# Hybrid attention and S5 layer, FFN: residual stores in GpSimd's queue, three operand splits on GpSimd, and a step of one pair as eight plain products

## The chip, the cores and the metric

The kernel runs on one core of a Trainium2 chip. The metric is the device time of one execution in microseconds (us), from the median of several runs. The engines are named as the profile names them: PE (TensorE matmuls, with PEld for its weight loads), DVE (VectorE), ACT (ScalarE), POOL (GpSimd) and SP (SyncE, which issues most DMAs).

## What is computed

One layer of a hybrid decoder on 1024 prompt positions and 8 sample positions (1032 columns in all), width 1024, with a feed-forward width of 2816. The part that matters here comes after the merge of the two branches:

```python
x = x + merged @ w_out
h2 = rms_norm(x, norm2_g)
x = x + (jax.nn.silu(h2 @ w_ffn_gate) * (h2 @ w_ffn_up)) @ w_ffn_down
y = rms_norm(x, norm_f_g)
```

All of it is float32 in and out. The kernel keeps everything transposed: 128 features on the partitions and the 1032 positions along the free axis.

## The kernel before

**Arithmetic.** Each float32 operand is split into a rounded high part (a cast to fp32r on ACT) and the rest, the low part (a subtraction, on DVE as a rule), and a product is three matmuls: high times high, high times low, low times high. So a weight block becomes usable in three steps: SP loads it (`wr_...`), ACT casts it (`wh_...`), DVE subtracts (`wl_...`). The casts and subtractions write to rings of three buffers, the raw blocks to rings of three (`wraw`) or seven (`hsm`).

**Positions.** They are cut into two stretches s = 0 and 1 of 516 columns (`SC`), each of two halves of 258 (`HC`). A matmul here has 258 columns.

**Output projection, `wout(s)`.** For each of eight row blocks m: two weight loads, the residual `xres`, 48 matmuls, the sum in `X1[m]` (tile `mg`) on DVE, its square on ACT, the sum of squares `s2`, and a DMA of the stretch of `X1[m]` to the DRAM tile `x1d`, which is read again in the last part. In the code before, SP issues that DMA, so in SP's queue it stands between the loads of the following weight blocks. `operands(s)` then scales `X1` in place by the norm (L1178), forms the sums `ts` and splits them into the operands `ho`. `wout(1)` runs woven with `operands(0)`, and `light(0)`, the first products of the FFN for stretch 0, with `operands(1)`.

**Seven products.** The two FFN projections and the down projection are computed in 2x2 blocks by a scheme of seven products for eight (`seven`, `products`): four row blocks of weights a11, a12, a21, a22, three sums and differences of them on POOL (`ws1` to `ws4` are four instructions), seven splits on ACT and DVE, and seven evictions of PSUM into the result. `combine` makes the seven right-hand sides of the down projection out of the four blocks of the hidden layer b11, b12, b21, b22; `spill` writes them to DRAM (`hid0` to `hid6`).

**Down projection.** `STEP` groups the eleven pairs of hidden row blocks into six steps, the last of which, step 5, has one pair (pair 1). `load_step(h)` reads the step's seven right-hand sides back (`hr`, a ring of three buffers) and splits them (`do`: a high part on ACT, a low part on DVE). `DOWN` lists which rows m of the result take which steps: `(2, 0, 1)` and `(3, 0, 1)` come first (tiles `d02`, `d03`), with step 1 loaded meanwhile, and `(2, 5, 6)` and `(3, 5, 6)` (tiles `d52`, `d53`) are the step of one pair for the rows m = 2 and 3; then come `(0, 4, 6)` and the last row, `(1, 4, 6)`. `down_after` adds each product to `X` on DVE, and where a row is done it squares it on ACT, sums the squares on POOL (tile `s`, 128x1032) and scales it on ACT.

**What sets the order.** Each engine runs its own queue in order. The queues are laid out at build time by a scheduler that simulates the program, so an edit at one place can exchange instructions around it.

Of the kernel before, what the change touches and what calls it, by code (L numbers as in the profile page):

```python
# [29 lines left out]
SC = 516  # L30
# [27 lines left out]
def body_(ctx, tc, h, o):  # L58
# [972 lines left out]
    hidd = [[dram.tile([128, SC], F32, tag=f"hid{i}_{f}", name=f"hid{i}_{f}") for f in range(NP)] for i in range(7)]  # L1031
    x1d = [dram.tile([128, T], F32, tag=f"x1d{m}", name=f"x1d{m}") for m in range(KD)]
# [106 lines left out]
    def wout(s):  # L1139
        cs = stretch(s)  # L1140
        for m in range(KD):
# [14 lines left out]
            SY.dma_start(x1d[m][:, cs], X1[m][:, cs])  # L1156
# [48 lines left out]
    def spill(f, U, ts, sl):  # L1205
        for i, src in enumerate(combine(U, ts, (P, V, P, V))):
            SY.dma_start(hidd[i][f].rearrange("p (s t) -> p s t", s=2)[:, sl], src)

# [117 lines left out]
    def load_step(h_):  # L1326
# [3 lines left out]
        for i in (range(7) if h_ != 1 else (2, 4, 6, 0, 3, 5, 1)):  # L1330
# [3 lines left out]
            for k in range(n):  # L1334
                SY.dma_start(t[:, k], hidd[i][fs[k]].rearrange("p (s t) -> p s t", s=2))
            tags = POS[h_ % 2]
            if n == 1:
                o_ = buf(tags[i], f"do{nm}", F32R, (128, 2, 2, HC))
                hi, lo = o_[:, 0:1], o_[:, 1:2]
            else:  # L1340
                hi, lo = (buf(tags[2 * i + e], f"do{nm}{'hl'[e]}", F32R, (128, 2, 2, HC)) for e in range(2))
            ops[h_, i] = hi, lo
            S.copy(hi, t[:, 0:n])
            V.tensor_tensor(lo, t[:, 0:n], f32(hi), op=ALU.subtract)
# [8 lines left out]

    sqs = {}
    started = []

    def down_after(m, last):
        xa, xb = tok(X[m]), tok(X[m + 4])

        def run(i, ps, sl):  # L1360
# [3 lines left out]
            if last and i >= 5:  # L1364
                j = m + 4 * (i - 5)
                if m != LASTM:
                    if not started:
                        started.append(j)
                        S.activation(s3, X[j], AF.Square)
                    else:  # L1370
                        sq = buf("s2", f"sq3{j}")
                        S.activation(sq, X[j], AF.Square)
                        P.tensor_tensor(s3, s3, sq, op=ALU.add)
                    S.activation(X[j], X[j], AF.Copy, scale=gf[:, j:j + 1])
                else:
                    s = sl.start
                    sqs[s, j] = small(f"sq3{j}{s}").rearrange("p a b -> p (a b)")
                    S.activation(sqs[s, j], X[j][:, stretch(s)], AF.Square)
# [66 lines left out]
    for n, (m, a, b) in enumerate(DOWN):  # L1445
# [6 lines left out]
        nm = f"d{a}{m}"  # L1452
        products(seven(down_rows(m, fs), 128 * len(fs), nm), down_op(a, b), (0, 1), nm,
# [122 lines left out]
```

## Time and profile before

| | |
|---|---|
| median of 3 runs | 1423.12 us (1421.62 to 1427.08) |
| profiled execution, its time | 1422.4 us |
| its span, first to last instruction | 1420.6 us |
| mean granted clock of PE | 0.972 of full speed |
| busy share PE, DVE, ACT, POOL | 95%, 64%, 40%, 33% |

Matmuls are pipelined and their ends are modelled, so PE's busy share hides small waits. The number of matmuls that began in a stretch of given length, beside the granted clock, tells more: a stretch where PE runs without a pause shows how many fit. A row of a timeline ends in brackets where its engine had been idle before it, with the time and what ended it.

### The profile page before, as it was taken

The page shows a single profiled execution, that of the slowest core. Times are in us where ns is not written, and L with a number is a line of the kernel's source. Part 1 is how long each engine was busy: PE and PEld are TensorE (multiplying, and loading weights), DVE is VectorE, ACT ScalarE, POOL GpSimd, SP SyncE. Part 2 cuts the span into 40 slices and gives each one's busy share as a digit, 9 for nine tenths or more (in the row PEclk, how much of TensorE's full clock was granted, in tenths as well). Part 3 has the DMA queues.
Part 4 walks back from the last instruction along what each step waited for, and adds up shares of the span by engine and source line. Part 5 has one row for each costly group of instructions (what it writes and reads, how often), then busy time and mean ns, then how long its engine had stood idle before and what let it go on. Part 6 is the DMA issues. An engine that isn't in the chain of part 4 may idle for free.

```text
span 1420.6 us, 25988 instructions
## 1 busy us (share of the span) xinstructions
PE 1342.8 (95%) x10019; PEld 1308.4 (92%) x10019; DVE 913.6 (64%) x1831; ACT 566.3 (40%) x1124; POOL 472.5 (33%) x431
## 2 busy tenths in 40 slices
PE   8999999987789999998899999999999979999995
PEld 7999999977689999997899999999999879999985
DVE  7968864389998545537394444444434896777593
ACT  6125655233236423334353333333334552344351
POOL 3033221266770001017063333333333552332153
PEclk9999999998789999999999999999999999999997
DMA  7230001211112011453443233323223863544113
GB/s 287 88 114 30 17 23 31 62 48 32 32 25 72 23 46 45 124 182 120 140 128 118 101 105 112 105 98 105 83 91 112 269 203 126 157 150 131 48 40 120
DMA packets 89931, 140.01 MB, mean 99 GB/s; under 512 B 16328, under 2 KB 33232, under 8 KB 89808
## 3 DMA queue, kind: packets, MB, share of 16 engines
q1 hardware_dynamic: 88448, 135.02, 30.1%
q0 software_dynamic: 640, 2.10, 0.4%
q8 instruction: 79, 1.29, 0.4%
q10 hardware_dynamic: 720, 1.23, 0.2%
q14 instruction: 44, 0.36, 0.1%
HBM read 104.90 MB, written 32.22 MB: 97 GB/s over the span
## 4 chain that ended last, share of the span: by engine, by line
PE 65%; DVE 12%; DMA 2%; issue 2%; POOL 1%; ACT 1%; SPq 0%; DVEq 0%; ACTq 0%; POOLq 0%
PE gs L130 2%; PE gs L128 2%; PE gs L129 2%; PE wo L130 2%; PE wo L128 2%; PE wo L129 2%; PE ps L128 1%; PE ps L130 1%; PE ps L129 1%; DVE mg L923 1%; PE pa L128 1%; PE pa L129 1%; PE pa L130 1%; DVE mg L1178 1%; DVE RE L873 1%
## 5 line engine op out<-in xcount | busy, mean ns | idle before, releaser
L130 PE MATMUL wo<-mh,wl_wo 128*128 128x258 f32 x256 | 74.0, 290 | 5.3 <-DVE wl_wo L118 5.3
L128 PE MATMUL wo<-mh,wh_wo 128*128 128x258 f32 x256 | 74.0, 289 | 2.4 <-ACT wh_wo L117 1.7
L129 PE MATMUL wo<-ml,wh_wo 128*128 128x258 f32 x256 | 73.2, 286 | 0.0
L130 PE MATMUL gs<-xh,wl_gs 128*128 128x344 f32 x192 | 62.2, 327 | 5.0 <-DVE wl_gs L118 5.0
L129 PE MATMUL gs<-xl,wh_gs 128*128 128x344 f32 x192 | 62.1, 324 | 0.0
L128 PE MATMUL gs<-xh,wh_gs 128*128 128x344 f32 x192 | 62.0, 324 | 0.0
L1094 POOL TENSOR_TENSOR ws_u<-wr_1u,ws_u 128x512 f32<-128x512 f32 x11 | 14.2, 1287 | 125.3 <-issue 125.3
L130 PEld LDWEIGHTS wo<-mh,wl_wo 128*128 128x128 f32 x256 | 49.5, 194 | 5.9 <-DVE wl_wo L118 5.9
L1094 POOL TENSOR_TENSOR ws_d<-wr_1d,ws_d 128x512 f32<-128x512 f32 (+3 forms) x14 | 15.3, 1090 | 117.6 <-DVE wl_3d L1081 56.5
L128 PEld LDWEIGHTS wo<-mh,wh_wo 128*128 128x128 f32 x256 | 49.9, 195 | 3.1 <-ACT wh_wo L117 3.1
L129 PEld LDWEIGHTS wo<-ml,wh_wo 128*128 128x128 f32 x256 | 49.7, 194 | 0.0
L118 DVE TENSOR_TENSOR wl_wo<-wr_wo,wh_wo 128x512 fp32r<-128x512 f32 x32 | 23.5, 735 | 39.8 <-ACT wh_wo L117 39.8
L130 PE MATMUL ga<-xh,wl_ga 128*128 128x344 f32 x144 | 47.1, 327 | 1.8 <-DVE wl_ga L118 1.8
L128 PE MATMUL ga<-xh,wh_ga 128*128 128x344 f32 x144 | 47.5, 330 | 0.0
L129 PE MATMUL ga<-xl,wh_ga 128*128 128x344 f32 x144 | 47.0, 326 | 0.0
L495 POOL TENSOR_TENSOR ml<-mg,mh 128x344 fp32r<-128x344 f32 x6 | 6.7, 1147 | 115.3 <-ACT mh L494 115.3
L130 PEld LDWEIGHTS gs<-xh,wl_gs 128*128 128x128 f32 x192 | 36.7, 192 | 5.2 <-DVE wl_gs L118 5.2
L577 ACT ACTIVATE P<-P,st 128x256 f32<-128x256 f32 (+1 forms) x64 | 31.0, 486 | 17.7 <-DVE st L574 17.7
L128 PEld LDWEIGHTS gs<-xh,wh_gs 128*128 128x128 f32 x192 | 36.6, 191 | 0.0
L117 ACT CAST wh_wo<-wr_wo 128x512 fp32r<-128x512 f32 x32 | 19.8, 619 | 42.2 <-PE wo L129 40.2
L129 PEld LDWEIGHTS gs<-xl,wh_gs 128*128 128x128 f32 x192 | 36.6, 191 | 0.0
L202 PE MATMUL u<-xh,wuh 128*128 128x344 f32 x96 | 30.8, 326 | 4.2 <-ACT wuh L220 4.0
(2689 smaller groups left out, 5863.1 us busy)
## 6 DMA issues: line engine op xcount, KB each, us to landing
hr<-hid SPq DMA_DIRECT2D x77, 258.0 KB, 3.5
wr_wo<-in_wout SPq DMA_DIRECT2D x32, 256.0 KB, 2.9
xres<-in_xT SPq DMA_DIRECT2D x16, 258.0 KB, 3.6
x1d<-mg SPq DMA_DIRECT2D x16, 258.0 KB, 2.8
x<-x1d SPq DMA_DIRECT2D x8, 516.0 KB, 4.7
wr_ga<-in_wst SPq DMA_DIRECT2D x16, 256.0 KB, 2.6
wr_gs<-in_wst SPq DMA_DIRECT2D x16, 256.0 KB, 2.6
wr_0g<-in_wfg SPq DMA_DIRECT2D x15, 256.0 KB, 3.0
```

The lines of the kernel that those rows point to most:

```text
L117: S.copy(wh[:, 0:w], raw[:, 0:w])
L118: (eng or V).tensor_tensor(wl[:, 0:w], raw[:, 0:w], f32(wh[:, 0:w]), op=ALU.subtract)
L128: TE.matmul(ps, wh, xh[:, cs], start=(k == 0), stop=False)
L129: TE.matmul(ps, wh, xl[:, cs], start=False, stop=False)
L130: TE.matmul(ps, wl, xh[:, cs], start=False, stop=(k == n - 1))
L202: TE.matmul(ps[:, :CH], wh, XH[k][:, chunk(c)], start=(k == 0), stop=False)
L495: eng.tensor_tensor(lo, src, f32(hi), op=ALU.subtract)
L577: S.activation(Pt[:, i, 0:W], Pt[:, i, 0:W], AF.Exp, bias=nm_[:, i:i + 1], scale=0.125, accum_out=ds[:, i:i + 1])
L873: V.tensor_tensor_scan(RE[:, gg], a, W1[:, gg], 0.0, op0=ALU.mult, op1=ALU.add)
L923: V.tensor_tensor(MG[m][:, chunk(c)], MG[m][:, chunk(c)], t, op=ALU.mult)
L1094: P.tensor_tensor(t, x, y, op=op)
L1178: V.scalar_tensor_tensor(x, x, g2[:, j:j + 1], r2[:, cs], op0=ALU.mult, op1=ALU.mult)
```

## The change

Four things are done.

1. In `wout`, the store of `X1[m]` to `x1d` is issued by POOL and not by SP.
2. In `load_step(1)`, the low parts of the right-hand sides 4, 0 and 5 are subtracted on POOL; the other four stay on DVE.
3. The step of one pair is no longer computed by seven products for the rows m = 2 and 3 (`d52`, `d53`) but by `plain`: eight products, four row blocks of weights as they are, two halves of columns, each output block the sum of two products in its own PSUM tile. No sum of weights is formed, there are four splits and four evictions for a row where there were seven of each, and the two rows take 96 matmuls of 258 columns where there were 84.
4. The plain products need b12, which the scheme of seven products does not keep: it is spilled for pair 1 to a new DRAM tile `h12` (one DMA for each stretch), and loaded and split as an eighth right-hand side of step 5.

```diff
-            SY.dma_start(x1d[m][:, cs], X1[m][:, cs])
+            P.dma_start(x1d[m][:, cs], X1[m][:, cs])
...
             SY.dma_start(hidd[i][f].rearrange("p (s t) -> p s t", s=2)[:, sl], src)
+        if f in STEP[-1]:
+            SY.dma_start(h12.rearrange("p (s t) -> p s t", s=2)[:, sl], U[1])
...
-        for i in (range(7) if h_ != 1 else (2, 4, 6, 0, 3, 5, 1)):
+        for i in (range(7 if n > 1 else 8) if h_ != 1 else (2, 4, 6, 0, 3, 5, 1)):
...
-                SY.dma_start(t[:, k], hidd[i][fs[k]].rearrange("p (s t) -> p s t", s=2))
+                SY.dma_start(t[:, k], (hidd[i][fs[k]] if i < 7 else h12).rearrange("p (s t) -> p s t", s=2))
...
             S.copy(hi, t[:, 0:n])
-            V.tensor_tensor(lo, t[:, 0:n], f32(hi), op=ALU.subtract)
+            (P if h_ == 1 and i in (4, 0, 5) else V).tensor_tensor(lo, t[:, 0:n], f32(hi), op=ALU.subtract)
...
+    def plain(m, a, after):
+
+        n = 128
+        nm = f"d{a}{m}"
+        w = []
+        for q, ld in enumerate(down_rows(m, STEP[a])):
+            t = raw512(f"{q}{nm}")
+            ld(t)
+            w.append(wsplit(t[:, 0:n], n, f"{q}{nm}"))
+            if q % 2 == 0:
+                continue
+            for c in range(2):
+                t = two(("b0", "b1", "b0", "b2")[q - 1 + c], f"{nm}{q}{c}")
+                for s in range(2):
+                    for e in range(2):
+                        i = ((0, 1), (7, 5))[c][e]
+                        mm(t[:, s, 0:HC], w[q - 1 + e], lambda k: tuple(x[:, 0, s] for x in ops[a, i]), e == 0, e == 1)
+                after(q // 2, c, t[:, :, 0:HC])
...
+    def plain_after(m):
+        def run(r, c, ps):
+            d = tok(X[m + 4 * r])[:, :, c]
+            V.tensor_tensor(d, ps, d, op=ALU.add)
+            if c:
+                squares(m, r, slice(0, 2))
+        return run
...
         nm = f"d{a}{m}"
+        if len(fs) == 1:
+            plain(m, a, plain_after(m))
+            continue
         products(seven(down_rows(m, fs), 128 * len(fs), nm), down_op(a, b), (0, 1), nm,
```

`squares` is what `down_after` did at the end of a row, moved into a function of its own.

The scheduler moves instructions at the places below. The first is ACT's queue in `wout(1)`, where the row blocks m = 5 and 6 (`wo51`, `wo61`, each loaded in a part 0 and a part 512) are cast between the high parts `ho` of `operands(0)`. Before:

```order
L1184 CAST ho2h0_7161<-ts20_7351 128x258
L1154 ACTIVATE sq231_7345<-mg3_2896 128x516
L1184 CAST ho6h0_7169<-ts20_7351 128x258
L1184 CAST ho3h0_7163<-ts30_7440 128x258
L117 CAST wh_wo51_512_7467<-wr_wo51_512_7465 128x512
L1184 CAST ho4h0_7165<-ts30_7440 128x258
L1184 CAST ho2h0_7161<-ts30_7440 128x258
L117 CAST wh_wo61_0_7529<-wr_wo61_0_7527 128x512
```

And with the change, on the same engine at the same place:

```order
L1185 CAST ho2h0_7162<-ts20_7352 128x258
L1155 ACTIVATE sq231_7346<-mg3_2896 128x516
L1185 CAST ho6h0_7170<-ts20_7352 128x258
L117 CAST wh_wo51_512_7468<-wr_wo51_512_7466 128x512
L1185 CAST ho3h0_7164<-ts30_7441 128x258
L117 CAST wh_wo61_0_7530<-wr_wo61_0_7528 128x512
L1185 CAST ho4h0_7166<-ts30_7441 128x258
L1185 CAST ho2h0_7162<-ts30_7441 128x258
```

The cast of the second part of block 5 now stands ahead of the first cast that reads `ts30`, and that of block 6 two places further ahead; DVE's subtractions for them move in the same way.

On POOL, at the same place, the sums `ts20` and their low parts stood in a row before:

```order
L1066 TENSOR_TENSOR ts10_7262<-mg5_2902,ts10_7262 128x258
L1067 TENSOR_TENSOR ts10_7262<-mg5_2902,ts10_7262 128x258
L1185 TENSOR_TENSOR ho2l0_7162<-ts10_7262,ho2h0_7161 128x258
L1185 TENSOR_TENSOR ho6l0_7170<-ts10_7262,ho6h0_7169 128x258
L1064 TENSOR_TENSOR ts20_7351<-mg2_2895 128x258
L1065 TENSOR_TENSOR ts20_7351<-mg6_2903,mg2_2895 128x258
L1066 TENSOR_TENSOR ts20_7351<-mg6_2903,ts20_7351 128x258
L1067 TENSOR_TENSOR ts20_7351<-mg6_2903,ts20_7351 128x258
L1185 TENSOR_TENSOR ho2l0_7162<-ts20_7351,ho2h0_7161 128x258
L1185 TENSOR_TENSOR ho6l0_7170<-ts20_7351,ho6h0_7169 128x258
L1064 TENSOR_TENSOR ts30_7440<-mg3_2896 128x258
```

With the change, POOL's queue there reads:

```order
L1067 TENSOR_TENSOR ts10_7263<-mg5_2902,ts10_7263 128x258
L1157 DMA x1d2_6452<-mg2_2895 128x516
L1068 TENSOR_TENSOR ts10_7263<-mg5_2902,ts10_7263 128x258
L1186 TENSOR_TENSOR ho2l0_7163<-ts10_7263,ho2h0_7162 128x258
L1186 TENSOR_TENSOR ho6l0_7171<-ts10_7263,ho6h0_7170 128x258
L1065 TENSOR_TENSOR ts20_7352<-mg2_2895 128x258
L1066 TENSOR_TENSOR ts20_7352<-mg6_2903,mg2_2895 128x258
L1067 TENSOR_TENSOR ts20_7352<-mg6_2903,ts20_7352 128x258
L1068 TENSOR_TENSOR ts20_7352<-mg6_2903,ts20_7352 128x258
L1157 DMA x1d3_6453<-mg3_2896 128x516
L1186 TENSOR_TENSOR ho2l0_7163<-ts20_7352,ho2h0_7162 128x258
L1186 TENSOR_TENSOR ho6l0_7171<-ts20_7352,ho6h0_7170 128x258
```

Two stores stand between the sums, one of them ahead of the last sum of `ts10`, the other ahead of the low parts of `ts20`.

The second place is SP's queue at the end of `wout(1)`, with the last residuals and the first weights of the FFN (`wr_0g000` and on). Before:

```order
L1156 DMA x1d5_6454<-mg5_2902 128x516
L1144 DMA xres61_7539<-in_xT 128x516
L1156 DMA x1d6_6455<-mg6_2903 128x516
L1144 DMA xres71_7607<-in_xT 128x516
L1156 DMA x1d7_6456<-mg7_2904 128x516
L1256 DMA wr_0g000_7666<-in_wfg 128x512
L1256 DMA wr_1g000_7672<-in_wfg 128x512
```

With the change, on SP at the same place:

```order
L111 DMA wr_wo71_512_7602<-in_wout 128x512
L1145 DMA xres61_7540<-in_xT 128x516
L1145 DMA xres71_7608<-in_xT 128x516
L1259 DMA wr_0g000_7667<-in_wfg 128x512
L1259 DMA wr_1g000_7673<-in_wfg 128x512
```

No instruction that waits for a result of DVE is left ahead of the first FFN weights in SP's queue.

The third place is DVE's queue at the start of the down projection (`d02`), where the low parts of step 1 (`do14l`, `do10l`, `do16l`) stand between the last products of the hidden layer (`A15`, `s2`), the weight splits and the evictions `x22`. Before:

```order
L1081 TENSOR_TENSOR wl_0d02_13254<-wr_0d02_13249,wh_0d02_13253 128x256
L1344 TENSOR_TENSOR do14l_13211<-hr14_13207,do14h_13210 128x1032
L1227 TENSOR_TENSOR A15_11_12839<-A15_11_12839,h6_11_12838 128x258
...
L1363 TENSOR_TENSOR x22_13134<-d02b0_13257,x22_13134 128x2x258
L1344 TENSOR_TENSOR do10l_13225<-hr10_13221,do10h_13224 128x1032
L1065 TENSOR_TENSOR s2_11_12840<-A15_11_12839 128x258
L1344 TENSOR_TENSOR do16l_13218<-hr16_13214,do16h_13217 128x1032
L1363 TENSOR_TENSOR x22_13134<-d02b1_13275,x22_13134 128x2x258
L1081 TENSOR_TENSOR wl_3d02_13315<-ws1_d02_13293,wh_3d02_13314 128x256
```

With the change, on DVE:

```order
L1082 TENSOR_TENSOR wl_0d02_13257<-wr_0d02_13252,wh_0d02_13256 128x256
L1230 TENSOR_TENSOR A15_11_12841<-A15_11_12841,h6_11_12840 128x258
...
L1066 TENSOR_TENSOR s2_11_12842<-A15_11_12841 128x258
L1082 TENSOR_TENSOR wl_2d02_13301<-ws2_d02_13298,wh_2d02_13300 128x256
L1409 TENSOR_TENSOR x22_13137<-d02b0_13260,x22_13137 128x2x258
L1068 TENSOR_TENSOR s2_11_12842<-A15_11_12841,s2_11_12842 128x258
L1347 TENSOR_TENSOR do16l_13221<-hr16_13217,do16h_13220 128x1032
L1409 TENSOR_TENSOR x22_13137<-d02b1_13278,x22_13137 128x2x258
L1082 TENSOR_TENSOR wl_3d02_13318<-ws1_d02_13296,wh_3d02_13317 128x256
```

`do14l` and `do10l` are gone from DVE's queue ahead of the fourth weight split, and the last sum `s2` of the hidden layer stands ahead of `do16l`. POOL takes `do14l` ahead of its first sum `s2`, `do10l` ahead of its weight sum `ws4`, and `do15l` after the weight sums of `d03`.

## Rows read from the trace of the kernel before

**Rows 1.** Page, part 1: busy time, share of the span, instructions.

```profile
PE 1342.8 (95%) x10019; PEld 1308.4 (92%) x10019; DVE 913.6 (64%) x1831; ACT 566.3 (40%) x1124; POOL 472.5 (33%) x431
```

**Rows 2.** Stretches: length, busy PE PEld DVE ACT POOL (x started), clock, DMA share, GB/s.

```profile
585.00:590.00 5.00, 5.00 (x44) 5.00 (x44) 1.98 (x3) 1.88 (x3) 0.00 (x0) 1.00 0.33 104
...
670.00:675.00 5.00, 5.00 (x30) 5.00 (x30) 3.52 (x5) 1.82 (x4) 1.83 (x3) 0.66 0.66 211
...
690.00:695.00 5.00, 2.38 (x15) 2.30 (x15) 2.10 (x6) 1.86 (x4) 0.00 (x0) 0.65 0.97 315
695.00:700.00 5.00, 5.00 (x31) 5.00 (x31) 1.02 (x4) 1.93 (x3) 0.00 (x0) 0.67 0.54 191
```

**Rows 3.** The same view in stretches of 10 us, down projection.

```profile
1160.00:1170.00 10.00, 6.03 (x39) 5.49 (x38) 9.40 (x13) 5.09 (x8) 6.45 (x6) 0.80 0.86 258
...
1190.00:1200.00 10.00, 10.00 (x86) 10.00 (x85) 4.95 (x8) 1.87 (x3) 5.16 (x4) 1.00 0.18 51
...
1350.00:1360.00 10.00, 7.95 (x56) 6.85 (x55) 9.33 (x18) 7.24 (x15) 5.13 (x6) 1.00 0.29 80
1360.00:1370.00 10.00, 8.86 (x63) 8.89 (x64) 9.83 (x14) 6.18 (x10) 5.53 (x4) 0.83 0.21 59
```

**Rows 4.** Chain of waits that ended last: start, us, engine, tile, line.

```profile
667.09 0.65 POOL ts L1064
668.08 0.62 ACT wh_wo L117
668.72 1.04 DVE wl_wo L118
...
688.31 4.00 DMA wr_0g<-in_wfg
```

**Rows 5.** PE's timeline around block 5 and at the FFN's start: start, us.

```profile
667.29 0.28 PE L130 MATMUL wo<-mh,wl_wo 128*128 128x258 f32 x1
668.75 0.39 PE L128 MATMUL wo<-mh,wh_wo 128*128 128x258 f32 x1 [1.17 <-ACT wh_wo L117]
668.97 0.28 PE L129 MATMUL wo<-ml,wh_wo 128*128 128x258 f32 x1
669.81 0.39 PE L130 MATMUL wo<-mh,wl_wo 128*128 128x258 f32 x1 [0.56 <-DVE wl_wo L118]
...
689.41 1.05 PE L157 MATMUL r2c<-ones,s 128*86 128x2 f32 x12 [2.28 <-DVE s L1155]
...
693.08 0.58 PE L1115 MATMUL xg<-ho0h,wh_0g 128*128 128x258 f32 x1 [2.62 <-ACT wh_0g L1080]
```

**Rows 6.** ACT's timeline, the cast ahead of block 5's second part.

```profile
667.76 0.41 ACT L1184 CAST ho3h<-ts 128x258 fp32r<-128x258 f32 x1 [2.51 <-POOL ts L1064]
```

**Rows 7.** POOL's timeline: a DMA that it issues, and its longest wait.

```profile
8.79 0.54 POOL L217 DMA_DIRECT2D wur<-in_wu  x1 [4.68 <-DVE wul L225]
...
653.52 4.91 POOL L1065 TENSOR_TENSOR ts<-mg,mg 128x258 f32<-128x258 f32 x1
```

**Rows 8.** Who PE waited for from 1105 to 1182 us: total, times, longest.

```profile
PE d02b L1117 <- DVE wl_3d L1081: 2.3, 1, 2.3
PE d02b L1115 <- DVE x L1363: 2.1, 2, 1.7
```

**Rows 9.** Timelines of DVE and POOL: a split of step 1, and a DVE split beside a POOL sum.

```profile
1157.01 1.22 DVE L1344 TENSOR_TENSOR do14l<-hr,do14h 128x1032 fp32r<-128x1032 f32 x1
...
1365.21 2.78 DVE L1081 TENSOR_TENSOR wl_2d<-ws_d,wh_2d 128x384 fp32r<-128x384 f32 x1
...
1365.05 2.52 POOL L1373 TENSOR_TENSOR s<-s,sq 128x1032 f32<-128x1032 f32 x1 [2.58 <-ACT sq L1372]
```

**Rows 10.** DVE's timeline in the step of one pair: a split, an eviction, an undisturbed 384 split.

```profile
1348.29 0.28 DVE L1081 TENSOR_TENSOR wl_2d<-ws_d,wh_2d 128x128 fp32r<-128x128 f32 x1
1348.48 0.69 DVE L1363 TENSOR_TENSOR x<-d52b,x 128x516 f32<-128x516 f32 x1
...
1364.28 0.55 DVE L1081 TENSOR_TENSOR wl_1d<-wr_1d,wh_1d 128x384 fp32r<-128x384 f32 x1
```

More of the change, by code (lines that the diff above doesn't have):

```diff
@@ L1031, in body_ @@
     hidd = [[dram.tile([128, SC], F32, tag=f"hid{i}_{f}", name=f"hid{i}_{f}") for f in range(NP)] for i in range(7)]
+    h12 = dram.tile([128, SC], F32, tag="h12", name="h12")
     x1d = [dram.tile([128, T], F32, tag=f"x1d{m}", name=f"x1d{m}") for m in range(KD)]
@@ L1334, in load_step @@
             for k in range(n):
-                SY.dma_start(t[:, k], hidd[i][fs[k]].rearrange("p (s t) -> p s t", s=2))
+                SY.dma_start(t[:, k], (hidd[i][fs[k]] if i < 7 else h12).rearrange("p (s t) -> p s t", s=2))
             tags = POS[h_ % 2]
             if n == 1:
-                o_ = buf(tags[i], f"do{nm}", F32R, (128, 2, 2, HC))
+                o_ = buf(tags[i] if i < 7 else ("r", "Zh3", "Zh2")[nraw[0] % 3], f"do{nm}", F32R, (128, 2, 2, HC))
                 hi, lo = o_[:, 0:1], o_[:, 1:2]
@@ L1352, in down_op, with squares @@
         return op
+    def plain(m, a, after):
[15 more added lines that the diff above has]
+                after(q // 2, c, t[:, :, 0:HC])
     sqs = {}
     started = []
+    def squares(m, i, sl):
+        j = m + 4 * i
+        if m != LASTM:
+            if not started:
+                started.append(j)
+                S.activation(s3, X[j], AF.Square)
+            else:
+                sq = buf("s2", f"sq3{j}")
+                S.activation(sq, X[j], AF.Square)
+                P.tensor_tensor(s3, s3, sq, op=ALU.add)
+            S.activation(X[j], X[j], AF.Copy, scale=gf[:, j:j + 1])
+        else:
+            s = sl.start
+            sqs[s, j] = small(f"sq3{j}{s}").rearrange("p a b -> p (a b)")
+            S.activation(sqs[s, j], X[j][:, stretch(s)], AF.Square)
+    def plain_after(m):
[5 more added lines that the diff above has]
+        return run
     def down_after(m, last):
@@ L1364, in run @@
             if last and i >= 5:
[L1365 to L1378, printed above, removed]
+                squares(m, i - 5, sl)
         return run
```

## The prediction

> **What bounds the kernel now.** I read the page's busy shares first [rows 1]: PE is busy for 95% of the span, so the other engines matter only where PE stands still or runs at half clock. The stretches show where. A full 5 us, 585 to 590, takes 44 matmuls of 258 columns [rows 2]; a full 10 us, 1190 to 1200, takes 86 [rows 3]: 0.116 us for one. Three places that the change touches fall short, and each has its own last wait.
>
> Place A is the second stretch of the output projection and the start of the FFN behind it. From 670 to 675 us PE began 30 matmuls at a mean clock of 0.66, from 690 to 700 us 15 and 31 at 0.65 and 0.67 [rows 2]; such a mean is a mixture of the two levels, 2.4 GHz (1.00) and 1.2 GHz (0.50), and each time PE had paused before it. The chain of waits runs there through a POOL sum, an ACT cast and a DVE split between 667 and 669 us [rows 4], and then through the landing of the first FFN weight, issued at 688.31 us and 4.00 us in coming. PE's timeline shows the two pauses that these end [rows 5]. Place B is the start of the down projection, 1160 to 1170 us: 39 of 86 matmuls, clock 0.80, DVE busy 9.40 of 10 us [rows 3]. The waits name DVE both times, once for a weight split and twice for evictions [rows 8]. Place C is the step of one pair, 1350 to 1370 us: 56 and 63 of 86 with DVE at 9.33 and 9.83 [rows 3].
>
> **Part 1, the stores, at block 5.** ACT's cast for block 5's second part stood behind a cast that waited 2.51 us for POOL's `ts30` [rows 6]. PE paused from 667.29 to 668.75 and from 668.97 to 669.81 us [rows 5], 2.30 us in all, of which two ordinary steps of 0.12 are work: 2.06 lost. In the new order the cast stands ahead of that wait, and only behind `ho6h` of `ts20`. Against that, POOL's queue has two stores among the sums. An issue took POOL 0.54 us [rows 7], and both sums that they store are on time, so the sums come up to 1.1 us later. I trace it through: the casts and the split are then ready some 0.5 us after PE wants them. So 1.5 us of the 2.06 come back. The half clock behind the pause cost 14 matmuls against 44 in 5 us, 1.6 us; with a quarter of the pause left I take 1.5 of it (0 to 1.6).
>
> **Part 1, at the FFN's start.** SP's queue no longer holds the store of block 7, which waited for DVE, ahead of `wr_0g000`. The load needs a free buffer of the ring of seven, and the one it takes was last read for block 4, three blocks earlier; so it lands under block 6 or 7. What is late next is the sum of squares: PE began its column sums at 689.41 us, after 2.28 us of waiting for DVE, and they take 1.05 us [rows 5]. So the first FFN product can start at 690.5 and not at 693.08: 2.6 us. DVE's first split stands behind a small operation on those column sums and ends some 0.9 us after them (0.2 and 0.7, as the 516 columns of [rows 10]), 0.4 late for PE's fifth matmul: 2.2 us remain. The half clock after 693.08 us costs 9 matmuls for 16 up to 695 us (the other 6 of the 15 are column sums) and 31 for 44 after it [rows 2], together 20 at 0.116, 2.3 us. The pause shrinks to a shorter one; I take 1.0 (0 to 2.3). The stores of the first stretch, and the last ones, find POOL idle and cost nothing. If POOL were busy there, 0.54 us each would count. The two further DMAs for `h12` and its load are three issues among SP's others, whose cover is the loads that wait for buffers anyway; 0. Without the cover they would cost about 1 us.
>
> Part 1 together: 1.5 + 1.5 + 2.2 + 1.0 = 6.2 us.
>
> **Part 2, the three splits.** DVE sheds three splits of 1.22 us [rows 9], 3.7 us in a stretch where it has no time left. POOL takes 2.52 us for an operation of that size, and the same rows show what DVE pays beside it: a split that takes 0.55 us alone [rows 10] took 2.78, from 1365.21 to just after POOL's end at 1367.57 us. So POOL's operation holds DVE's next split until it is over. The Trainium skill, SBUF — State Buffer, section Who interferes with whom, gives this as a rule: a DVE instruction with two SBUF inputs and a GpSimd instruction that reads SBUF contend for one exclusive lock, and the later one blocks until the first is done. That speaks against this part, and the trace agrees: 2.78 against 0.55 us; evictions, which read PSUM, are free of it (0.69).
>
> I walk the queues with these durations. `do14l` on POOL falls beside DVE's first weight split of `d02` and holds it until PE has waited some 0.8 us. `do10l` falls beside the sum `s2` and `do16l`, holds them for about 2.4 us, and the fourth weight split, for which PE waits now, comes some 1.8 us later than now. What comes back: the third eviction, for which PE waits 1.7 us [rows 8], no longer stands behind `do13l`, and two later evictions not behind `do11l` and `do15l`. By that count PE's fifth product starts about when it does now, and a shorter pause behind it goes. Net I take 0, between a loss of 2.5 (both holds, nothing back) and a gain of 3.7 (no hold).
>
> **Part 3, the plain products.** The stage loses 30 + 23 matmuls in 1350 to 1370 us [rows 3]: 53 x 0.116 = 6.1 us. The change adds 12 matmuls, 1.4 us. DVE drops six splits of 0.28 us and six evictions of 0.69 [rows 10], 5.8 us in a stage of 16, and POOL eight small sums. PE then is the longer side: 96 matmuls are 11.2 us, DVE's eight splits and eight evictions 7.8. What stays is one hold by POOL's sum of squares, up to 2.5 us [rows 9], since the last split of `d53` falls beside it; I take 2.4. Gain 6.1 - 1.4 - 2.4 = 2.3 us (1.0 to 4.7). The split of the eighth right-hand side, 0.7 us on DVE, falls under the last product of `d33`, where DVE still has pauses.
>
> **Sum.** Against the profiled execution, 1422.4 us: 1422.4 - 6.2 - 0 - 2.3 = 1413.9. The median of the runs shown, 1423.12, is 0.7 higher, so the forecast is 1414.5. A measurement of this kernel tells about 0.5% (7 us) from no change; the forecast is 8.6 below the median, close to that bound.
>
> **The rivals.** *Half of it.* Pauses get shorter but the clock falls as often as now, and in the step of one pair ACT, which squares and scales the finished rows between the casts, is the new wait, so that part 3 only pays for its own matmuls. For it: a pause of 2.3 us ahead of the column sums stays [rows 5], and a shorter one, 1.46 us, sufficed for the half clock of 670 to 675 us. Against it: ACT was busy 7.24 and 6.18 of 10 us [rows 3] and sheds six casts. Then 1422.4 - 1.5 - 2.2 = 1418.7, with the median 1419.
>
> *All of it.* DVE's splits find POOL's pauses, part 2 pays 3.7 us, no hold stays in part 3 (4.7), and the clock stays up (1.5 + 1.6 + 2.2 + 2.3): 16.0 us, so 1406.4. For it: DVE and POOL overlap without loss in many rows. Against it: rows 9.
>
> *Slower: the stores hold POOL.* POOL's longest operation of its kind, 4.91 us [rows 7], where another of these sums took 0.65 [rows 4], began just as DVE started a run of splits without a pause, and ended when DVE paused. If an issue is held like that, the stores of blocks 1, 2 and 3, which fall in that run, cost 3 x (4.9 - 0.5) = 13 us in the chain POOL, ACT, PE [rows 4], and a further half-clock stretch some 1.6 us: 1414.5 + 14.6 = 1429; from about 3.3 us a store the change is a loss. Against it: an issue at 8.79 us took 0.54 [rows 7].
> The same page of the Trainium skill, section SBUF: two separate sides, warns of this, and the section A bandwidth-pool intuition that's wrong has the figure: a DMA issued from GpSimd whose descriptors wait for DVE takes about 3.1 us where it takes 0.62 alone; by that figure three stores would cost 7.4 us (an estimate from the page) and the time would be about 1422. It ties this to a mode of DVE that its two-input operations don't have, and no row here shows a GpSimd issue beside busy DVE.
>
> **How the numbers follow.** Forecast 0.49, its own range 1410 to 1417. Half of it 0.24. All of it 0.14. Slower 0.13. Faster by over 0.5% is below 1416: 0.42 of the forecast's share and all of the third, 0.56. Slower by over 0.5% is above 1430: half of the fourth, 0.07. The rest, 0.37, is within 0.5%. The range 1408 to 1421 leaves out the fourth case and half of the third, 0.20.
>
> **What would show it.** Part 1: the first FFN product starts within 1.5 us of the column sums' end, no pause over 0.7 us in block 5, each store on POOL near 0.54 us. Wrong if stores take 2 us or more beside DVE, or if the first weight still lands last. Part 2: POOL's `do` rows near 2.5 us with DVE rows of 1.5 us or more beside them, and PE's matmuls of 1160 to 1170 us between 35 and 50 of 86. Part 3: the 96 matmuls of `d52` and `d53` in 12 to 14 us where the 84 took 16. The forecast is wrong altogether if one of the earlier gains turns up as a new wait later: in the last row, whose DVE is full.

## The result and the profile after

The changed kernel takes 1414.25 us, median of 4 runs (1413.53 to 1415.45), where the kernel before takes 1423.26: a ratio of 0.9934 with a 95% interval of 0.9913 to 0.9955, or 9.0 us. A second measurement, beside other runs of the kernel before, gives 1414.89 against 1421.93, ratio 0.9951 (0.9938 to 0.9964), or 7.0 us. The forecast was 1414.5, and 8.5 us for the sum.

Single executions of one kernel differ by more than a part of this change is worth: the kernel before ran from 1415.1 to 1427.4 us. The traces show one reason, and it matters for what follows: the stretches in which PE is granted half its clock do not fall at the same places in each execution. So the parts are read stage by stage, from several traces, and not from totals alone.

The page of the changed kernel, part 1, answers to [rows 1]:

```profile
PE 1340.5 (95%) x10031; PEld 1306.4 (92%) x10031; DVE 907.2 (64%) x1817; ACT 565.8 (40%) x1119; POOL 483.3 (34%) x442
```

PE has 12 matmuls more and 2.3 us less of busy time, since less of it runs at half clock. POOL is busy 10.8 us longer: it has sixteen stores and three splits more, and eight small sums fewer.

Place A, PE's timeline of the changed kernel around block 5 and at the FFN's start, answers to [rows 5]:

```profile
668.63 0.39 PE L130 MATMUL wo<-mh,wl_wo 128*128 128x258 f32 x1 [0.53 <-DVE wl_wo L118]
...
686.70 1.05 PE L157 MATMUL r2c<-ones,s 128*86 128x2 f32 x12 [2.27 <-DVE s L1156]
687.61 0.37 PE L1116 MATMUL xg<-ho0h,wh_0g 128*128 128x258 f32 x1
...
688.61 0.58 PE L1118 MATMUL xg<-ho0h,wl_0g 128*128 128x258 f32 x1 [0.28 <-DVE wl_0g L1082]
```

Of block 5's two waits, 1.17 and 0.56 us, one of 0.53 is left. The first FFN product follows the column sums without a wait; what remains there is 0.28 us for DVE's split. The pause of 2.27 us ahead of the column sums is what it was. POOL's timeline shows the stores that came into its queue, with a row of DVE's timeline that runs beside the second of them, and SP's timeline the first FFN weights:

```profile
658.88 0.57 POOL L1157 DMA_DIRECT2D x1d<-mg  x1
665.03 0.56 POOL L1157 DMA_DIRECT2D x1d<-mg  x1
...
664.41 1.23 DVE L118 TENSOR_TENSOR wl_wo<-wr_wo,wh_wo 128x512 fp32r<-128x512 f32 x1
...
671.22 0.56 POOL L1157 DMA_DIRECT2D x1d<-mg  x1
...
685.45 0.54 POOL L1157 DMA_DIRECT2D x1d<-mg  x1 [5.18 <-DVE mg L1150]
```

```profile
673.73 0.33 SPq L1259 DMA_DIRECT2D wr_0g<-in_wfg  x1
676.34 0.33 SPq L1259 DMA_DIRECT2D wr_0g<-in_wfg  x1
```

The first weight is issued at 673.73 us, under block 6, 14 us ahead of its use; before it was 688.31 [rows 4].

Place B, PE's pauses in `d02` and `d03` (answers to [rows 8]), then POOL's low parts of step 1 and the DVE rows that run beside them (answers to [rows 9]):

```profile
1153.13 0.39 PE L1118 MATMUL d02b<-do00h,wl_0d 128*128 128x258 f32 x1 [0.50 <-DVE wl_0d L1082]
1156.96 0.36 PE L1116 MATMUL d02b<-do02h,wh_2d 128*128 128x258 f32 x1 [0.95 <-DVE x L1409]
1160.88 0.39 PE L1118 MATMUL d02b<-do03h,wl_3d 128*128 128x258 f32 x1 [1.99 <-DVE wl_3d L1082]
1167.28 0.39 PE L1118 MATMUL d03b<-do00h,wl_0d 128*128 128x258 f32 x1 [0.41 <-DVE wl_0d L1082]
1169.89 0.39 PE L1118 MATMUL d03b<-do01h,wl_1d 128*128 128x258 f32 x1 [0.92 <-DVE wl_1d L1082]
1172.58 0.39 PE L1116 MATMUL d03b<-do02h,wh_2d 128*128 128x258 f32 x1 [0.97 <-DVE x L1409]
```

```profile
1149.96 2.84 POOL L1347 TENSOR_TENSOR do14l<-hr,do14h 128x1032 fp32r<-128x1032 f32 x1
...
1155.89 2.57 POOL L1347 TENSOR_TENSOR do10l<-hr,do10h 128x1032 fp32r<-128x1032 f32 x1
...
1167.15 2.41 POOL L1347 TENSOR_TENSOR do15l<-hr,do15h 128x1032 fp32r<-128x1032 f32 x1 [2.87 <-ACT do15h L1346]
```

```profile
1150.80 2.28 DVE L1082 TENSOR_TENSOR wl_0d<-wr_0d,wh_0d 128x256 fp32r<-128x256 f32 x1
...
1156.74 2.01 DVE L1068 TENSOR_TENSOR s<-A,s 128x258 f32<-128x258 f32 x1
...
1167.75 2.08 DVE L1082 TENSOR_TENSOR wl_1d<-wr_1d,wh_1d 128x256 fp32r<-128x256 f32 x1
```

The same split with no POOL row beside it, of the same timeline:

```profile
1160.42 0.41 DVE L1082 TENSOR_TENSOR wl_3d<-ws_d,wh_3d 128x256 fp32r<-128x256 f32 x1
```

Each of POOL's three rows holds one DVE row until its own end: 2.28, 2.01 and 2.08 us for operations of 256 or 258 columns that take 0.41 alone. Each hold has its pause on PE. The pauses sum to 5.7 us in these rows, where the waits named in [rows 8] sum to 4.4. Yet the stage is not longer, and the stretches say why (10 us each; PE, PEld, DVE, ACT, POOL busy, clock):

```profile
1150.00:1160.00 10.00, 7.02 (x53) 6.22 (x51) 10.00 (x14) 3.43 (x6) 6.68 (x4) 1.00 0.76 224
1160.00:1170.00 10.00, 7.79 (x61) 7.37 (x62) 8.24 (x13) 5.20 (x9) 5.70 (x5) 1.00 0.98 314
...
1340.00:1350.00 10.00, 10.00 (x86) 9.88 (x84) 5.32 (x12) 5.92 (x10) 1.09 (x2) 1.00 0.36 102
1350.00:1360.00 10.00, 7.69 (x59) 7.07 (x59) 10.00 (x11) 6.36 (x10) 7.03 (x4) 1.00 0.18 53
1360.00:1370.00 10.00, 10.00 (x86) 10.00 (x85) 8.65 (x12) 4.27 (x8) 8.62 (x6) 1.00 0.01 2
```

From 1150 to 1170 us the clock is 1.00; before it was 0.80 in the stretch with the pauses [rows 3]. Place C is in the last three rows: 86 of 86 matmuls while the plain products run, then 59, then 86 again, where [rows 3] had 56 and 63. The loss has moved behind the plain products, to the start of row 0 (timelines of PE, DVE, POOL and ACT):

```profile
1351.35 0.39 PE L1116 MATMUL d40b<-do40h,wh_0d 128*128 128x258 f32 x1 [0.64 <-ACT wh_0d L1081]
1355.07 0.39 PE L1118 MATMUL d40b<-do40h,wl_0d 128*128 128x258 f32 x1 [1.55 <-DVE wl_0d L1082]
...
1352.29 2.73 DVE L1082 TENSOR_TENSOR wl_0d<-wr_0d,wh_0d 128x384 fp32r<-128x384 f32 x1
...
1351.91 2.69 POOL L1388 TENSOR_TENSOR s<-s,sq 128x1032 f32<-128x1032 f32 x1
...
1350.38 0.51 ACT L1081 CAST wk_0d<-wr_0d 128x384 fp32r<-128x384 f32 x1 [0.46 <-DMA wr_0d<-in_wfd]
```

The two pauses have different causes. The 1.55 us end with DVE's split, which POOL's sum held for 2.73 us. The 0.64 us end with ACT's cast `wh_0d`, which follows the cast `wk_0d` of the same weight, and that one waited for the weight to land.

### The profile page after: what moved, and what is told of

Its sections match the earlier page's. It is cut to its first block, busy times and chain, and to the rows that moved or that the text cites. A ratio compares the mean times of both kernels' runs of the same rounds, so it can differ in the third digit from the quotient of the medians.

```text
span 1412.4 us, 25976 instructions
## 1 busy us (share of the span) xinstructions
PE 1340.5 (95%) x10031; PEld 1306.4 (92%) x10031; DVE 907.2 (64%) x1817; ACT 565.8 (40%) x1119; POOL 483.3 (34%) x442
## 3 DMA queue, kind: packets, MB, share of 16 engines
q8 instruction: 79, 1.29, 0.4%
## 4 chain that ended last, share of the span: by engine, by line
PE 63%; DVE 13%; issue 3%; DMA 2%; POOL 1%; ACT 1%; SPq 0%; DVEq 0%; ACTq 0%; POOLq 0%
PE gs L130 2%; PE gs L128 2%; PE gs L129 2%; PE wo L130 2%; PE wo L128 2%; PE wo L129 2%; PE ps L128 1%; PE ps L130 1%; PE ps L129 1%; DMA hr<-hid 1%; DVE mg L923 1%; PE pa L128 1%; PE pa L129 1%; PE pa L130 1%; DVE mg L1179 1%
## 5 line engine op out<-in xcount | busy, mean ns | idle before, releaser
L1095 POOL TENSOR_TENSOR ws_u<-wr_1u,ws_u 128x512 f32<-128x512 f32 x11 | 14.2, 1290 | 125.0 <-issue 125.0
L1095 POOL TENSOR_TENSOR ws_d<-wr_1d,ws_d 128x512 f32<-128x512 f32 (+2 forms) x12 | 14.4, 1197 | 102.0 <-DVE wl_3d L1082 57.7
L117 ACT CAST wh_wo<-wr_wo 128x512 fp32r<-128x512 f32 x32 | 19.8, 619 | 38.9 <-PE wo L129 35.8
L1157 POOL DMA_DIRECT2D x1d<-mg x16 | 8.9, 556 | 74.3 <-DVE mg L1150 74.3
```

The lines of the kernel that those rows point to most:

```text
L117: S.copy(wh[:, 0:w], raw[:, 0:w])
L1095: P.tensor_tensor(t, x, y, op=op)
L1157: P.dma_start(x1d[m][:, cs], X1[m][:, cs])
```

## The experiments

Fourteen traces were read: the two above and twelve more, ten of them of further kernels and two of the same two kernels again. Three groups share their runs of the kernel before: the first four, the next four and the last four.

**Stores alone.**

```diff
-            SY.dma_start(x1d[m][:, cs], X1[m][:, cs])
+            P.dma_start(x1d[m][:, cs], X1[m][:, cs])
```

> The kernel before with part 1 alone: the stores of the output projection in POOL's queue. Theory (the parts add up, as the trace of the changed kernel reads stage by stage): PE's column sums come 2.6 us earlier than before, the first FFN product 5.4 us, the FFN's products behind the half clock 5.7 us; the time falls by 5.7 us, and the half clock of 6.8 us in d02 is there as before. Rival (the half clock in d02 went because the place is reached 5.8 us earlier, not because of the splits): the time falls by some 7.5 us and no half clock shows in d02. Rival (stores hold POOL): single stores of 2 us or more, a gain under 3 us.

Measured: ratio 0.9966 (0.9950 to 0.9981), 4.8 us of 1419.9. In the trace PE comes from the first column sums to the second 2.66 us sooner than before, and the first FFN product follows 0.91 us behind the start of the second sums. The half clock in `d02` is there. No store took longer than 0.59 us. The gain is 0.9 below the 5.7 expected, which still lies within the interval (2.7 to 7.1 us). One reason is that the 5.7 counted on a half clock behind block 5 in the kernel before; the next two traces, with the stores still in SP's queue, have none there. The profiled execution was the slowest of the 13, 1422.75 us; the plain products below show where it lost its time.

**Splits alone.**

```diff
-            V.tensor_tensor(lo, t[:, 0:n], f32(hi), op=ALU.subtract)
+            (P if h_ == 1 and i in (4, 0, 5) else V).tensor_tensor(lo, t[:, 0:n], f32(hi), op=ALU.subtract)
```

> The kernel before with part 2 alone: three low parts of step 1 on POOL. Theory: d02 and d03 get 1.3 us more of PE's pauses, in shorter pieces, and lose the half clock of 6.8 us, so from the first product of d02 to the first of d00 it takes 28.0 us for 28.85, and the time falls by 0.8 us. Rival (the half clock went for another reason): it stays, and the time rises by about 1.3 us. In both, DVE splits beside POOL's three rows take 2.0 to 2.3 us where they take 0.41.

Measured: ratio 1.0004 (0.9988 to 1.0019), not apart from no change in the total. In the trace there is no half clock from `d02` to `d00`, and PE's pauses there sum to 6.1 us. To the first product of `d00`, the mark of the expectation, it takes 28.05 us, where 28.0 was expected; to the long run of `d00`, the mark used from here on, 29.72. So the theory's mechanism stands for this trace. Its 0.8 us rest on one trace of the kernel before, 28.85 us; the second trace of it, told below, has 28.25. The total neither bears out the 0.8 us nor excludes them.

**Plain products alone** (with the spill and the eighth right-hand side that they need; the edit is the third and fourth part of the diff ahead).

> The kernel before with part 3 alone: eight plain products for the rows 2 and 3 of the step of one pair, with the spill and the load that they need. Theory: the 96 matmuls run without a pause, 11.2 us for 15.9, and a hold of 2.7 us on DVE beside POOL's sum of squares, with 2.2 us of pauses on PE, shows up at the start of row 0: the time falls by 1.8 us. Rival (the hold's place is luck of the other parts, and the pause brings the clock down): no pause at row 0 and a gain of 4, or a stretch at half clock behind it and a gain under 0.5 us.

Measured: ratio 0.9989 (0.9972 to 1.0007), 1.6 us, by the total not apart from no change. From the last product of `d33` to the long run of `d41` it takes 35.55 us where the kernel before takes 37.55. The stage gains what was expected, and the hold is there: a split of 2.74 us on DVE, with pauses of 0.60 and 1.50 us on PE. The total of the profiled execution gains nothing like it, because its end is 4.4 us longer: from the long run of `d41` on it takes 42.9 us where the kernel before takes 38.5. The trace with the stores alone has the same long end, 42.7; all other traces lie between 38.3 and 39.3. The stretch that tells the two apart, of the kernel with the stores alone and then of the kernel before:

```profile
1390.00:1395.00 5.00, 5.00 (x25) 5.00 (x25) 1.52 (x6) 0.74 (x2) 0.00 (x0) 0.50 0.00 0
```

```profile
1390.00:1395.00 5.00, 5.00 (x51) 5.00 (x51) 2.44 (x11) 0.32 (x2) 0.00 (x0) 1.00 0.00 0
```

PE has no pause in either, and the code of that end is the same. The clock falls at 1388 us in the one and at 1401 in the other.

**All but the splits.**

```diff
-            (P if h_ == 1 and i in (4, 0, 5) else V).tensor_tensor(lo, t[:, 0:n], f32(hi), op=ALU.subtract)
+            V.tensor_tensor(lo, t[:, 0:n], f32(hi), op=ALU.subtract)
```

> The changed kernel with part 2 undone: all low parts of step 1 on DVE. Theory (the parts add up): 7.5 us below the kernel before, 0.8 above the changed kernel, and a half clock stretch stands in d02 again. Rival (the splits cost 1.3 us, and the half clock went because the place is reached earlier): 9.5 us below the kernel before, no half clock in d02.

Measured: ratio 0.9948 (0.9932 to 0.9963), 7.4 us, against 7.5 expected, with a half clock in `d02`, so the rival falls. Beside the stores alone, 0.9966 in the same group, that leaves 2.6 us for the plain products. Against the changed kernel (0.9951 and 0.9934) the totals don't tell whether the splits pay.

**The two kernels again.**

> The kernel before again, for a second trace of it beside the single parts. Theory (what the single parts' traces have in common is the kernel, what differs between them is where half-clock stretches fall): from the first column sums to the FFN's products behind the seam it takes 66 us (the traces without part 1 had 66.5 and 65.4), d02 and d03 30.5 us to the first of d00 with a half clock in it, rows 2 and 3 of the last step to the first long run of row 1 37.5 us; the tail behind that takes either 38.5 or 42.7 us. If the tail takes 42.7 us here too, that ending belongs to no part of the change.

> The changed kernel again, beside the kernel before on one chip, with more executions. Theory: the stages read as in its first trace (part 1 4.7 to 5.8, part 2 0.7, part 3 2.0 us), so 7.4 to 8.5 us below the kernel before, a ratio of 0.994 to 0.995. Rival (part 2 costs, as the medians of the changed kernel without it and of the splits alone may say): 5 to 6 us below, 0.996.

Measured: the kernel before, ratio 0.9993 (0.9983 to 1.0003) against its own runs; its stages took 66.4, 29.9 and 38.9 us, and its end 38.9, so the long end did not show in a second trace without the change. It is tied to neither part either: the traces of the changed kernel and of all but the splits have both parts and end in 38.7 to 38.9 us. What brings it is open. The changed kernel 0.9951, 7.0 us, a little under the 7.4 to 8.5 of the theory. Its interval (5.1 to 8.8 us) holds both the theory and most of the rival's 5 to 6 us.

**Half sums of squares.**

```diff
-                P.tensor_tensor(s3, s3, sq, op=ALU.add)
+                for s in range(2):
+                    P.tensor_tensor(s3[:, stretch(s)], s3[:, stretch(s)], sq[:, stretch(s)], op=ALU.add)
```

> The changed kernel with POOL's sums of squares of the last part (128x1032) made as two instructions of 516 columns each. Theory (the pause of 1.55 us at the start of row 0 is DVE's split held until POOL's sum is over): the split beside it takes 1.2 to 1.5 us where it took 2.73, PE's two pauses at row 0 shrink from 2.2 to about 1 us, and the time falls by 1 us at most; a row of POOL takes 1.2 to 1.4 us. Rival (DVE would have been late there for its own work): the split takes 0.55 us but comes as late, and the pauses stay at 2.2 us.

Measured: ratio 0.9957 (0.9943 to 0.9970). The pause that was in question, in PE's timeline, and the split and the sums beside it:

```profile
1352.85 0.39 PE L1118 MATMUL d40b<-do40h,wl_0d 128*128 128x258 f32 x1 [0.42 <-DVE wl_0d L1082]
...
1351.14 1.66 DVE L1082 TENSOR_TENSOR wl_0d<-wr_0d,wh_0d 128x384 fp32r<-128x384 f32 x1
...
1350.76 3.18 POOL L1389 TENSOR_TENSOR s<-s,sq 128x516 f32<-128x516 f32 x2
```

The split takes 1.66 us where it took 2.73, and PE waits 0.42 where it waited 1.55 (1.29 in the second trace of the changed kernel). So the pause was POOL's hold. The other pause at row 0, 0.64 us, is still 0.55 and still ends with ACT's cast. But POOL needs 3.18 us for the two halves instead of 2.69, the next splits are held in their turn, two new pauses of 0.28 and 0.32 us follow, and neither the total nor the stage is shorter: from the last product of `d33` to the long run of `d41` it takes 35.94 us, where eight traces with the plain products and whole sums take 35.26 to 35.60. The theory of the pause holds; the gain that it promised is not there.

**Filling the pause ahead of the column sums.** The three added matmuls write to the tile of the column sums before these do; nothing reads them.

```diff
         rc = anyb(f"r2c{s}")[:, 0]
+        if s == 1:
+            for _ in range(3):
+                TE.matmul(rc[:, 0:HC], ones, X1[7][:, half(1, 0)], start=True, stop=True)
```

> The changed kernel with three matmuls of 258 columns more (of the last row block of X1 with ones, result not used) in the pause ahead of the second column sums. Theory (the half clock of 3.4 us behind that pause is there because PE stands still for 2.3 us): the pause is 1.2 us or less, no half clock follows it, and the first FFN products gain 0.9 us (78 matmuls for 86 in 690 to 700 us); the column sums start at most 0.3 us later. Rival (the column sums themselves, with two columns each, bring the clock down): the half clock stays, and the time is the same or up to 0.3 us more.

Measured: ratio 0.9924 (0.9911 to 0.9937), 1411.0 us, 3.9 us under the changed kernel in the same group, with intervals that just don't meet. The `x6` are the three added matmuls: each of these float32 matmuls is two records, as the six column sums are twelve. PE's timeline, then the stretch of 690 to 700 us of this kernel and of the changed one:

```profile
685.19 1.57 PE L1166 MATMUL r2c<-mg,ones 128*128 128x258 f32 x6 [0.79 <-DVE mg L1150]
686.60 1.07 PE L157 MATMUL r2c<-ones,s 128*86 128x2 f32 x12
```

```profile
690.00:700.00 10.00, 10.00 (x85) 10.00 (x85) 3.30 (x6) 5.17 (x10) 0.00 (x0) 1.00 0.47 145
```

```profile
690.00:700.00 10.00, 10.00 (x78) 10.00 (x77) 3.00 (x6) 4.60 (x8) 0.00 (x0) 0.91 0.43 128
```

The pause is 0.79 us instead of 2.27, the clock stays at 1.00, and from the first FFN product to the first matmul that spreads the norm it takes 12.19 us where six traces with all stores in POOL's queue and no fill took 13.3 to 14.2. So the rival falls: the column sums are the same and the half clock is gone. The stage gains 1.1 to 2.0 us; no single stage shows the rest of the 3.9, which may be the spread of executions. This is the fastest of the kernels that ran; together with the half splits, told below, it was not tried.

**Only the last store.**

```diff
-            SY.dma_start(x1d[m][:, cs], X1[m][:, cs])
+            (P if s == 1 and m == 7 else SY).dma_start(x1d[m][:, cs], X1[m][:, cs])
```

> The kernel before with one store moved: only that of the last row block of the second stretch (m = 7) is issued by POOL. Theory (the gain at the FFN's start comes from this one store, which stood ahead of the first FFN weights in SP's queue; the gain at block 5 from the other order of ACT's casts): the first FFN product starts 0.9 to 1.5 us after the start of the column sums, as in the changed kernel, where it took 3.6 us; the stretch from the first to the second column sums stays at 54.5 to 56.1 us; the time falls by 3 to 3.5 us. Rival (the loads are held by the earlier stores too, or land late for want of a buffer): the first product still waits for the landing of its weight and starts 2 us or more after the column sums start, a gain under 2 us.

Measured: ratio 0.9977 (0.9963 to 0.9991), 3.3 us. PE's timeline:

```profile
687.38 1.89 PE L157 MATMUL r2c<-ones,s 128*86 128x2 f32 x12 [2.27 <-DVE s L1155]
689.13 0.56 PE L1115 MATMUL xg<-ho0h,wh_0g 128*128 128x258 f32 x1
```

No wait is left ahead of `xg`. It starts 1.75 us after the column sums, later than the 0.9 to 1.5 expected and short of the rival's 2, since the column sums themselves ran at half clock here and took 1.89 us for 1.05. From the second column sums to the norm's spreading it takes 15.66 us, where 17.6 to 18.1 are usual without the part and 14.2 to 15.7 with all stores moved: one store of sixteen brings the gain at the FFN's start, less what the clock took in this execution. From the first to the second column sums it takes 54.53 us, as in two traces without any store moved.

**Half splits.**

```diff
-            (P if h_ == 1 and i in (4, 0, 5) else V).tensor_tensor(lo, t[:, 0:n], f32(hi), op=ALU.subtract)
+            if h_ == 1 and i in (4, 0, 5):
+                for s in range(2):
+                    P.tensor_tensor(lo[:, 0:n, s], t[:, 0:n, s], f32(hi)[:, 0:n, s], op=ALU.subtract)
+            else:
+                V.tensor_tensor(lo, t[:, 0:n], f32(hi), op=ALU.subtract)
```

> The changed kernel with POOL's three low parts of step 1 made as two instructions of 516 columns each. Theory (DVE is held for as long as one POOL instruction lasts): DVE's splits beside them take 1.0 to 1.6 us where they took 2.0 to 2.3, PE's waits in d02 and d03 sum to 1 to 2 us less than the 6.2 us of the changed kernel, and d02 to d00 takes 28.5 to 29.5 us. Rival (a second instruction on POOL holds DVE again, as the halves of the sums of squares did): the pauses move but their sum stays within 0.7 us, 29.5 to 30.5 us.

Measured: ratio 0.9941 (0.9920 to 0.9961), 1412.3 us. DVE's and POOL's timelines:

```profile
1149.58 1.17 DVE L1082 TENSOR_TENSOR wl_0d<-wr_0d,wh_0d 128x256 fp32r<-128x256 f32 x1
1150.68 1.53 DVE L1230 TENSOR_TENSOR A<-A,h 128x258 f32<-128x258 f32 x1
...
1148.73 3.19 POOL L1349 TENSOR_TENSOR do14l<-hr,do14h 128x516 fp32r<-128x516 f32 x2
```

The first split is free after 1.17 us where it took 2.28, and the second half holds the next operation of DVE instead, which nobody waits for yet. `d02` to `d00` takes 28.06 us, 1.4 to 1.7 less than the changed kernel's two traces; PE's pauses sum to 2.8 us. That is better than expected, and the other outcome than that of the halved sums; by these two runs it depends on which DVE row meets the second half. The scheduler also placed some DVE operations in another order, so the 1.5 us are not all the halves'. Fewer pauses did not keep the clock up: one of 2.00 us is left, and a half clock of 3.4 us begins 1.1 us behind it (PE's timeline, then the stretch):

```profile
1156.40 0.36 PE L1116 MATMUL d02b<-do02h,wh_2d 128*128 128x258 f32 x1 [2.00 <-DVE x L1413]
...
1150.00:1160.00 10.00, 7.91 (x53) 7.22 (x53) 10.00 (x15) 3.78 (x6) 8.12 (x8) 0.88 0.84 245
```

**Stores in ACT's queue.**

```diff
-            P.dma_start(x1d[m][:, cs], X1[m][:, cs])
+            S.dma_start(x1d[m][:, cs], X1[m][:, cs])
```

> The changed kernel with the 16 stores in ACT's queue instead of POOL's. Theory (what pays is that SP's queue is free of them; the new queue only has to reach the store without making anybody wait): the first FFN product starts 0.9 to 1.5 us after the column sums start here too; at block 5 ACT's casts carry three issues of about 0.5 us more, so the stretch from the first to the second column sums takes 53.4 to 56 us; the time is that of the changed kernel or up to 2 us more. Rival (the gain needs POOL): the first product starts 3 us or more after the column sums start.

Measured: ratio 0.9938 (0.9916 to 0.9960), 1413.0 us. The first FFN product starts 0.92 us behind the start of the column sums, and from the first to the second column sums it takes 52.31 us, 1.1 less than with POOL and under the 53.4 to 56 expected; the scheduler ordered other things differently here too, so that 1.1 is not all the queue's. POOL has no part in the gain at the FFN's start: what pays is that SP is free of the stores. An issue takes ACT 0.33 to 0.36 us, and the last one starts together with the square that waits for the same sum.

**Fill, without the splits** (the fill as above, the splits as in "all but the splits").

> The changed kernel with the three filling matmuls of the run before ahead of the second column sums, and with part 2 undone. Theory (the fill keeps the clock up, and the splits on POOL pay 0.5 us at most): no half clock behind the seam, d02 to d00 30 us or more with a half clock in it, and 10 to 11 us below the kernel before, within 1 us of the run with the fill and the splits (ratio 0.9924). Rival (the splits cost): a ratio of 0.991 or less. Rival (the fill's gain was luck): a half clock behind the seam again and a ratio of 0.995.

Measured: ratio 0.9939 (0.9923 to 0.9955), 8.7 us and not the 10 to 11 expected. The clock stays at 1.00 behind the column sums, 86 matmuls in 690 to 700 us; `d02` to `d00` takes 30.02 us with a half clock. So the fill's effect on the clock came a second time. The ratio lies 0.0015 above that of the fill with the splits, between the theory's 1 us and the 0.995 of the rival that calls the fill's gain luck: by the total neither is excluded. The rival by which the splits cost, 0.991 or less, is.

## Why the prediction was right, point by point

Four stages, each from the first matmul of a tile to that of another in PE's timeline, from all traces with and without the part (us; means in brackets). A run whose edit alters a stage itself is left out of that row: the fills and the stores in ACT's queue of the first two, the half splits of the third, the half sums of the fourth. The run with the last store alone counts as without in the first row and is left out of the second.

| stage | without | with | gain | forecast |
|---|---|---|---|---|
| block 5: first to second column sums | 54.53 to 56.08 (55.15), 5 traces | 53.42 to 53.47 (53.44), 6 | 1.7 | 3.0 |
| FFN start: second column sums to the norm's spreading | 17.57 to 18.11 (17.86), 4 | 14.25 to 15.70 (14.63), 6 | 3.2 | 3.2 |
| splits: `d02` to the long run of `d00` | 29.92 to 30.95 (30.25), 7 | 29.46 to 30.53 (29.89), 6 | 0.4 | 0 |
| plain: last product of `d33` to the long run of `d41` | 37.55 to 38.87 (38.12), 5 | 35.26 to 35.60 (35.44), 8 | 2.7 | 2.3 |

The gains sum to 8.0 us, the forecast to 8.5; the two measurements are 9.0 and 7.0. That the first of them ended 0.3 us from the forecast is luck: the same pair of kernels differs by 2.0 us from one measurement to the other, and 1.3 us too much at block 5 stand against 0.4 too little twice.

**Block 5, mis-sized.** The mechanism held: with ACT's cast ahead of the wait for POOL's `ts30`, 1.73 us of waits became 0.53. The half-clock term, 1.5 us, was read from one execution as if it always stood there. Three of five traces without the moved stores (that of the last store alone counts among them here) have no half clock behind block 5 and shorter pauses (0.48 to 0.57 and 0.56 us instead of 1.17 and 0.56 [rows 5]), 54.53 us in all; two have both, 56.08. So the part brings 1.1 or 2.6, not 3.0. In two of the three the half clock comes at the FFN's start instead, 10.2 us of it where the traces of the kernel before have 6.8.

**FFN start, right in sum.** The first product came 2.7 us nearer to the column sums' start, 2.6 were forecast, and the split that I put 0.4 us late for the fifth matmul cost 0.28 in three of the six traces, nothing in the others. That leaves 0.7 of the 3.2 for the clock, where 1.0 of 0 to 2.3 was taken. What this term depends on is the pause of 2.27 us ahead of the column sums, by the two runs with the fill: the change left it, the fill cut it to 0.79 us, and no half clock followed.

**Splits, right by two errors that cancel.** All three holds came, two of them where I walked them; the third (`do15l`, 0.92 us of PE) I had not seen, and the evictions' own 0.95 and 0.97 neither. Left out on the other side: with the splits on POOL, no half clock in the stage in five of six traces, where all seven without have one. Why is open. The pauses are more and shorter, but the longest is still 1.99 us beside 2.27 before, one of the six has the half clock with the same pauses, and so has the run with half splits, whose pauses sum to 2.8 us.

**Plain products, right, with the hold at another place.** I put it at the last split of `d53`; it fell on the first split of row 0 and cost PE 1.55 us, 1.26 to 1.66 over the traces, where I took 2.4. The 0.64 us ahead of it, the wait for row 0's first weight, I had not seen; with it the pauses are 2.2. The 53 lost matmuls of the sum hold a half clock that I did not name: each of the five traces without the part has one in this stage, as [rows 3] show with 0.83, and no trace with it.

**Signs.** Those named for part 1 came: no wait behind the column sums, none over 0.53 us in block 5, stores of 0.54 to 0.59 us. Of part 2 the holds came, but not the 35 to 50 matmuls from 1160 to 1170 us: 61 began there, and 53 in the 10 us before, at full clock. The 96 plain matmuls took 15.6 us from first to last with 24 of `d33` among them, 12.8 without these, within the 12 to 14 named. No gain came back as a wait in the last row: from the long run of `d41` on it takes 38.8 and 38.9 us in the two traces of the changed kernel, 38.5 and 38.9 in those of the kernel before.

**Rivals.** *The stores hold POOL* fell: sixteen issues took 0.54 to 0.59 us, the one at 665.03 beside a DVE split of two SBUF inputs that ran from 664.41 to 665.64. The Trainium skill, SBUF — State Buffer, section SBUF: two separate sides, ties its slow GpSimd issue to another kind of DVE operation; no row here shows a store beside that kind, so its 3.1 us are not tested. *Half of it* was right for the clock behind the FFN's start and wrong for ACT in the plain stage, where PE had no pause; the 0.64 us behind it end with an ACT cast, but one that waited for a weight to land, not for squares. *All of it* failed at the holds. The rule of the same page, section Who interferes with whom, agrees in these rows: 2.28, 2.01, 2.08 and 2.73 us beside POOL, and 1.17 and 1.66 where POOL's instruction is half as long.

**A last store where the gain lay.** I gave the gain at the FFN's start to one store, behind which the first weight stood; the run with that store alone bears it out.

## What to carry to other kernels

Look for the instruction in a DMA queue that waits for the last result of a stage: everything issued behind it starts late, and here moving that one instruction brought 3.3 us where all sixteen brought 4.8. ACT's queue served as well as POOL's. A GpSimd operation of 2.4 to 2.8 us held a two-input DVE operation until its own end in every case read here, so ask which DVE row it meets and who waits for that row, and try it in halves: one stage gained 1.4 to 1.7 us by it, the other nothing. Before a term for the clock goes into a sum, read it from more than one execution, and look at the pause ahead of it: three matmuls that nobody reads, in a pause of 2.3 us, gave back over 1 us.

## What was not expected of the hardware

The end of one and the same code took 38.3 to 39.3 us in twelve traces and 42.7 and 42.9 in two, 25 matmuls against 51 in the same 5 us. In the two, PE had been at work for over 10 us without a pause when the clock fell; in the other twelve it fell later, 1.6 to 3.2 us behind a pause of 1.1 us. And PE's half clock ahead of block 5 cost nothing where PE waits for DVE behind it anyway: with the moved stores that stage takes 53.42 to 53.47 us whether the half clock ahead lasts 3.4 or 6.8 us.
